# Adaptive average pooling on one core: every load issued as two transfers of 64 partitions each

## The chip, the cores and the metric

The kernel runs on one core of a Trainium2 chip. The metric is the device time of one execution in microseconds; the median of 3 timed runs of the kernel before is 333.51 us (333.32 to 333.81).

## The reference

The input `x` is float32 of 32 x 256 x 4096. Each row of 4096 values is cut into 256 windows, and each window is averaged:

```python
for i in range(output_size):                 # output_size = 256
    start = int(i * length / output_size)    # length = 4096
    end = int((i + 1) * length / output_size)
    result[:, :, i] = np.mean(x[:, :, start:end], axis=-1)
```

Since 4096 is a multiple of 256, each window has 16 values. The input is 134.2 MB, the output 8.4 MB.

## The kernel before

Batch and channels are flattened to 8,192 rows. A tile is 512 rows, 4 rows (64 KB) in each of the 128 partitions, so there are 16 tiles of 8.39 MB. For the first 15 tiles partition p owns the 60 rows from 60p on, and tile t takes rows 4t to 4t+3 of them (`x_many`); the last tile is the final 512 rows, 4 consecutive rows per partition (`x_last`). The tiles come from a pool `inpool` with two buffers, named `xin` in the profile.

For each tile, in the order of the loop:

- L73, SyncE's queue (SP): one DMA transfer loads the tile, 128 partitions x 64 KB. Its buffer is that of tile t-2, so the issue waits until the last reader of that buffer is done.
- L76, GpSimd (POOL): of the second half of the windows (512 of a partition's 1,024), it adds the last 8 values of each onto the first 8, in place.
- L81, VectorE (DVE): sums the first half of the windows over 16 values each. It waits for the load only.
- L84, VectorE: sums the second half of the windows over the 8 values that L76 left. It waits for POOL, and it is the last reader of the buffer.
- L87, ScalarE (ACT): multiplies the tile's 1,024 sums per partition by 1/16, in place.

Results are collected in `res_many` (15 tiles) and `res_last` (the last tile). The stores go through `store` (L58), also on SP's queue: `res_many` in one transfer of 7,680 KB, issued behind the last load, and `res_last` at the end in two, of 120 and of 8 partitions. All transfers are issued by SP, in the order of the program, to one DMA queue. Semaphores and waits are put in by the framework, by what an instruction reads and writes; the order within each engine is that of the program.

Of the kernel before, what the change touches and what calls it, by code (L numbers as in the profile page):

```python
# [1 line left out]

# [4 lines left out]


@with_exitstack
def kernel(  # L10
    ctx: ExitStack,
    tc: tile.TileContext,
    x: bass.AP,
    output_size: int,
    out: bass.AP,
):

    nc = tc.nc
    F32 = mybir.dt.float32
    X = mybir.AxisListType.X

    batch, channels, length = x.shape
    ob, oc, olen = out.shape
    assert ob == batch and oc == channels and olen == output_size
    assert length % output_size == 0
    window = length // output_size  # L30
    hw = window // 2
    inv_w = 1.0 / float(window)

    P = nc.NUM_PARTITIONS
    R = 4
    rows = batch * channels
    assert rows % (P * R) == 0
    ntiles = rows // (P * R)
    many = (ntiles - 1) * R
    cells = R * output_size  # L40
    m = cells // 2
    cols = R * length

    xr = x.rearrange("b c l -> (b c) l")
    orow = out.rearrange("b c o -> (b c) o")
    x_many = xr[0 : P * many, :].rearrange("(p r) l -> p (r l)", p=P, r=many)
    o_many = orow[0 : P * many, :].rearrange("(p r) o -> p (r o)", p=P, r=many)
    x_last = xr[P * many :, :].rearrange("(p r) l -> p (r l)", p=P, r=R)
    o_last = orow[P * many :, :].rearrange("(p r) o -> p (r o)", p=P, r=R)

    res_many = nc.alloc_sbuf_tensor("res_many", [P, (ntiles - 1) * cells], F32, align_bytes=256)
    res_last = nc.alloc_sbuf_tensor("res_last", [P, cells], F32, align_bytes=256)
    inpool = ctx.enter_context(tc.tile_pool(name="inpool", bufs=2))

    stored = nc.alloc_semaphore("stored")

    def store(out, in_):
        ins = nc.sync.dma_start(out=out, in_=in_)  # L58
        tc.no_tile_sem_insts.add(ins.ins.name)
        ins.then_inc(stored, 16)  # L60

    for t in range(ntiles):
        last = t == ntiles - 1
        xbuf = inpool.tile([P, cols + 64], F32, name="xin")
        off = 32 if last else 0
        flat = xbuf[:, off : off + cols]
        xin = flat.rearrange("p (o w) -> p o w", w=window)
        if last:
            res, base, src = res_last, 0, x_last
        else:  # L70
            res, base = res_many, t * cells
            src = x_many[:, t * cols : (t + 1) * cols]
        nc.sync.dma_start(out=flat, in_=src)  # L73
        if last:
            store(o_many, res_many[:, :])
        nc.gpsimd.tensor_add(  # L76
            out=xin[:, m:cells, 0:hw],
            in0=xin[:, m:cells, 0:hw],
            in1=xin[:, m:cells, hw:window],
        )  # L80
        nc.vector.reduce_sum(  # L81
            out=res[:, base : base + m], in_=xin[:, 0:m, :], axis=X
        )
        nc.vector.reduce_sum(  # L84
            out=res[:, base + m : base + cells], in_=xin[:, m:cells, 0:hw], axis=X
        )
        nc.scalar.mul(  # L87
            out=res[:, base : base + cells],
            in_=res[:, base : base + cells],
            mul=inv_w,  # L90
        )
    for lo, hi in ((0, 120), (120, P)):
        store(o_last[lo:hi, :], res_last[lo:hi, :])

    ctx.pop_all().close()
    tc.close()
    tc.compile()  # L97
    nc.sync.wait_ge(stored, 48)
    nc.sync.sem_clear(stored)


# [1 line left out]
_INS = ['x', 'output_size']  # L103
_OUTS = [((32, 256, 256), 'float32')]

_NUMBERS = {'output_size': 256}


# [26 lines left out]
```

## Time and profile before

| | |
|---|---|
| median of 3 runs | 333.51 us (333.32 to 333.81) |
| span of the profiled execution | 332.2 us, so the median lies 1.3 us above it |
| busy: DVE, POOL, ACT | 209.7 us (63%), 139.7 us (42%), 18.2 us (5%) |
| DMA | 142.61 MB in 2,599 packets, 99.4% of 16 engines' span |
| L76 (POOL), L81 (DVE), L84 (DVE), L87 (ACT), each per tile | 8.72, 8.69, 4.42, 1.06 us |
| issue of a load on SP (L73), median | 0.33 us |

The profile is that of one execution, and the time of that execution is known by its span; what lies around the span is the difference to the timed runs. In timeline lines the columns are start and duration in us, then engine, line, operation, what is written and read, and in brackets how long the engine idled before and what released it. In a table of stretches, each line has a window, its length, then for DVE, ACT and POOL the busy time with the number of instructions, the granted clock of TensorE (which is not used here), the mean busy share of the 16 DMA engines and the GB/s that they moved. "Landing" of a load is the moment at which its readers are released.

### The profile page before, as it was taken

To read this page: it belongs to the slowest core of one execution; us is meant where nothing else is said; L and a number is where in the kernel's file an instruction comes from. 1 tells how busy PE (TensorE), PEld (TensorE's weight loads), DVE (VectorE), ACT (ScalarE), POOL (GpSimd) and SP (SyncE) were. 2 spreads that over 40 slices of the span, in tenths; PEclk is the share of its full clock that TensorE was granted. 3 is DMA by queue.
4 is the path that set the end of the run, shared out by engine and by line. 5 is a ranking of instruction groups with operands and counts; after the bars stand their busy time and mean duration, and the time that the engine had idled before them with its cause. 6 is when DMAs were issued, how large, how long until landed. Compare 5 with 4: busy or idle time off the path is not lost.

```text
span 332.2 us, 160 instructions
## 1 busy us (share of the span) xinstructions
DVE 209.7 (63%) x32; ACT 18.2 (5%) x17; POOL 139.7 (42%) x20
## 2 busy tenths in 40 slices
DVE  0029396692939669392956939295683929578392
ACT  1000101000010100001010000101000010101001
POOL 0027090642709064370906337090633709063370
DMA  9898989989898999989898998989899998989897
GB/s 379 379 505 379 505 379 442 442 379 505 379 505 379 481 402 402 481 379 505 379 497 387 466 418 379 505 379 505 379 489 395 418 466 379 505 379 505 363 473 300
DMA packets 2599, 142.61 MB, mean 429 GB/s; under 512 B 295, under 2 KB 295, under 8 KB 423
## 3 DMA queue, kind: packets, MB, share of 16 engines
q1 hardware_dynamic: 2599, 142.61, 99.4%
HBM read 134.22 MB, written 8.39 MB: 429 GB/s over the span
## 4 chain that ended last, share of the span: by engine, by line
DMA 66%; POOL 18%; DVE 11%; POOLq 3%; issue 0%; ACT 0%; SPq 0%
DMA xin<-in_x_dram 66%; POOL xin L76 18%; DVE res_many L84 9%; POOLq L97 3%; DVE res_last L84 1%; ACT res_last L87 0%; SPq L73 0%; POOLq L76 0%
## 5 line engine op out<-in xcount | busy, mean ns | idle before, releaser
L76 POOL TENSOR_TENSOR xin<-xin 128x4096 f32<-128x4096 f32 x16 | 139.5, 8719 | 181.9 <-DMA xin<-in_x_dram 181.9
L81 DVE TENSOR_REDUCE res_many<-xin 128x512 f32<-128x8192 f32 x15 | 130.3, 8686 | 107.3 <-DMA xin<-in_x_dram 107.3
L84 DVE TENSOR_REDUCE res_many<-xin 128x512 f32<-128x4096 f32 x15 | 66.3, 4420 | 2.5 <-POOL xin L76 2.3
L87 ACT ACTIVATE res_many<-res_many 128x1024 f32<-128x1024 f32 x15 | 15.8, 1056 | 289.6 <-DVE res_many L84 289.6
L81 DVE TENSOR_REDUCE res_last<-xin 128x512 f32<-128x8192 f32 x1 | 8.7, 8686 | 6.6 <-DMA xin<-in_x_dram 6.6
L84 DVE TENSOR_REDUCE res_last<-xin 128x512 f32<-128x4096 f32 x1 | 4.4, 4420 | 0.2 <-POOL xin L76 0.2
L87 ACT ACTIVATE res_last<-res_last 128x1024 f32<-128x1024 f32 x1 | 1.1, 1056 | 18.8 <-DVE res_last L84 18.8
L87 ACT ACT_TABLE_LOAD x1 | 1.3, 1283 | 0.7 <-PEq L116 0.7
L116 POOL MEMSET const-float32-0.0<- 128x1 f32 x1 | 0.1, 99 | 0.2 <-issue 0.2
L116 POOL MEMSET const-bfloat16-1.0<- 128x1 bf16 x1 | 0.1, 102 | 0.0
L116 POOL MEMSET const-uint8-127<- 128x1 uint8 x1 | 0.1, 102 | 0.0
L116 POOL MEMSET const-float32-1.0<- 128x1 f32 x1 | 0.1, 99 | 0.0
## 6 DMA issues: line engine op xcount, KB each, us to landing
out_dram<-res_many SPq DMA_DIRECT2D x1, 7680.0 KB
out_dram<-res_last SPq DMA_DIRECT2D x1, 480.0 KB
xin<-in_x_dram SPq DMA_DIRECT2D x16, 25.3
out_dram<-res_last SPq DMA_DIRECT2D x1, 32.0 KB
```

Source lines behind the costliest of these rows:

```text
L76: nc.gpsimd.tensor_add(out=xin[:, m:cells, 0:hw], in0=xin[:, m:cells, 0:hw], in1=xin[:, m:cells, hw:window],)
L81: nc.vector.reduce_sum(out=res[:, base : base + m], in_=xin[:, 0:m, :], axis=X)
L84: nc.vector.reduce_sum(out=res[:, base + m : base + cells], in_=xin[:, m:cells, 0:hw], axis=X)
L87: nc.scalar.mul(out=res[:, base : base + cells], in_=res[:, base : base + cells], mul=inv_w,)
L97: tc.compile()
L116: nc = _bacc.Bacc("TRN2", target_bir_lowering=False, num_devices=1)
```

## The change

L73 issues two transfers instead of one: the first fills partitions 0 to 63 of the buffer, the second partitions 64 to 127. Bytes, buffers, order of the tiles and all compute instructions stay as they are. Lines below it move down by one, so L76, L81, L84 and L87 become L77, L82, L85 and L88, and the load is L74.

```diff
-        nc.sync.dma_start(out=flat, in_=src)
+        for a, b in ((0, P // 2), (P // 2, P)):
+            nc.sync.dma_start(out=flat[a:b, :], in_=src[a:b, :])
         if last:
             store(o_many, res_many[:, :])
```

## The prediction

> **What bounds the kernel now.** I read the page first: engine shares, DMA queue, chain.
>
> ```profile
> span 332.2 us, 160 instructions
> DVE 209.7 (63%) x32; ACT 18.2 (5%) x17; POOL 139.7 (42%) x20
> DMA packets 2599, 142.61 MB, mean 429 GB/s; under 512 B 295, under 2 KB 295, under 8 KB 423
> q1 hardware_dynamic: 2599, 142.61, 99.4%
> DMA xin<-in_x_dram 66%; POOL xin L76 18%; DVE res_many L84 9%; POOLq L97 3%; DVE res_last L84 1%; ACT res_last L87 0%; SPq L73 0%; POOLq L76 0%
> ```
>
> DVE works 63% of the span and POOL 42%, but the one DMA queue fills 99.4% of 16 engines' time. The chain names POOL and DVE for some 30%, because load t+2 is issued only when tile t has been reduced and its buffer is free. The question is whether that issue is ever late. The timeline and the stretches between landings answer it.
>
> ```profile
> 22.53 8.69 DVE L81 TENSOR_REDUCE res_many<-xin 128x512 f32<-128x8192 f32 x1 [22.53 <-DMA xin<-in_x_dram]
> 35.78 19.62 SPq L73 DMA_DIRECT2D xin<-in_x_dram  x2
> 41.83 8.69 DVE L81 TENSOR_REDUCE res_many<-xin 128x512 f32<-128x8192 f32 x1 [6.08 <-DMA xin<-in_x_dram]
> 61.17 8.69 DVE L81 TENSOR_REDUCE res_many<-xin 128x512 f32<-128x8192 f32 x1 [6.13 <-DMA xin<-in_x_dram]
> 293.08 8.69 DVE L81 TENSOR_REDUCE res_many<-xin 128x512 f32<-128x8192 f32 x1 [6.02 <-DMA xin<-in_x_dram]
> 312.96 8.69 DVE L81 TENSOR_REDUCE res_last<-xin 128x512 f32<-128x8192 f32 x1 [6.59 <-DMA xin<-in_x_dram]
> ```
>
> ```profile
> 80.60:293.10 212.50, 144.15 (x23) 11.62 (x11) 95.91 (x11) 1.00 1.00 434
> 313.00:330.40 17.40, 13.06 (x2) 1.06 (x1) 8.72 (x1) 1.00 0.92 398
> 330.40:331.60 1.20, 0.00 (x0) 0.00 (x0) 0.00 (x0) 1.00 0.95 389
> ```
>
> Load 2 is issued at 35.78 and load 1 lands at 41.83: the queue has 6 us of work left when new work arrives. Landings follow each other every (293.08 - 22.53) / 14 = 19.325 us, which for 8.39 MB is 434 GB/s, at a DMA share of 1.00 (last two columns). Behind the last landing the queue still has the 7,680 KB store of `res_many`, at 398 GB/s to 330.4; the last two stores follow at 389 GB/s to 331.6. So the whole span is one queue that is never empty: what matters is what the change does to the rate of the queue, and nothing else.
>
> **The change, part by part.** The built program lists 32 transfers of 64 x 16384 on SP where it had 16 of 128 x 16384; every other engine has the same instructions in the same order. So the change does what it says.
>
> SP: 16 more issues at 0.33 us each (L73's median). The second issue of a pair has no waits of its own, and comes 0.33 us behind the first, into the 6 us of slack: nothing on the path. Behind the last pair stands only the `res_many` store, whose rows wait behind the loads in the same queue anyway. If the slack were gone the price would be 16 x 0.33 = 5.3 us.
>
> Waits: L81 and L76 now wait for two landings. Between landing and start there are 0.02 to 0.11 us now; one more wait of that size per tile lies inside the 6 us that DVE idles before every L81. On the last tile it delays the last two stores, which queue behind `res_many`: DVE, POOL and ACT are done at 327.33, about 3 us before that store's rows run out at 330.4. Nothing.
>
> More packets: 295 small packets are 16 loads x 16, the `res_many` store's 16, 15 for the 120-row store and 8 for the 8-row one: one end mark per transfer and DMA engine used. The split adds 16 per engine. In the trace's packet records a row of 64 KB starts 2.414 us after the row before it, and 2.420 us where a load's end mark lies between: 6 ns each, 0.1 us in all.
>
> Start and completion: load 0 is issued at 0.73 and read at 22.53, so 21.80 - 19.325 = 2.48 us pass in start and completion. If none of it overlapped, 16 more transfers would cost 16 x 2.48 = 39.7 us; if the queue pipelines them as it pipelines loads now (cadence equal to the moving time), nothing. I take nothing, since two loads are already queued back to back without a gap.
>
> The rate of a 64-row transfer is the unknown. No transfer in the trace has 64 rows. Bounds from the nearest rows: a full load takes 19.325 us, 16 engines carrying 8 rows each, 27.1 GB/s an engine. If each engine keeps that pace with 4 rows per half, a half takes 9.66 us and the change costs nothing. If a transfer to half of the partitions has half of the ways into the memory, the 16 engines share them two by two, and a half takes the full 19.325 us: the bytes are halved and the time is not. The nearest smaller transfer is the 120-row store: 389 GB/s with 15 of 16 engines, against 15/16 of 434 = 407. That says that rate follows how much of the machine a transfer spans, but it is near the full end and cannot say which resource counts. A gain from the rate is excluded: the share is already 1.00 at 434.
>
> I take the upper end. At 128 rows each engine fills its own eight partitions without being slowed (2.42 us for nearly every row), which is what one separate way per engine looks like; with 64 rows the same 16 engines crowd on half of the partitions, and both halves run in order through the same queue, so the other half's ways stand empty meanwhile. All engines start together and get equal work, so nothing in the trace pulls them out of step.
>
> The Trainium skill, "SBUF — State Buffer", section "Door 1: The DMA port swizzle", says just this: partitions 0 to 63 reach only 8 of 16 DMA ports, with 196 GB/s measured at 1 MiB against 328 for 128 partitions; as an estimate from that page, its limit of about 218 GB/s would make the 134 MB of loads 616 us. "DMA: Bandwidth & Descriptors", "Rules for kernel authors", advises against two transfers to disjoint halves: they serialize. The trace agrees with those pages on the full-width rate (434 beside their 436), and shows no transfer that tests the half.
>
> The sum: 16 loads x 19.325 us more = 309.2. The tail of stores is unchanged. The span goes from 332.2 to 641.4; the timed median is 1.3 us above the span (333.51), so 642.7, and with the little that engines started some tenths of a microsecond apart may overlap, 642.
>
> **The rivals.**
>
> Not slower, 0.22: the destination sets no limit, each DMA engine does, and 4 rows + 4 rows are 8 rows. For it: the flat 27.1 GB/s an engine looks like the engine's own speed; and the tail at 389 GB/s shows no slow stretch although its last store has only 8 partitions, served by 8 engines at once. Against: that is 32 KB, which may be read ahead, and it is a store. Decided by whether two engines can write one group of partitions at full pace. Then 333.5 + 0.1 = 333.6, nothing in the chain moved, within the 0.2% (0.67 us) that a measurement here can tell from none.
>
> Partly overlapped, 0.13: the ways are halved, but one engine of a sharing pair gets ahead by half a load (9.66 us), and then the two work on opposite halves without meeting. Against: the lead cannot last. Load t+2 is issued when L84 of tile t ends, 13.2 us after the landing (41.83 to 55.06), so an engine 9.66 us ahead has run dry and waits 3.6 us, or up to 6.1 with 2.48 of start; call it 5. 333.5 + 9.7 + 15 x 5 = 418. It needs an uneven sharing between engines.
>
> Fixed cost not overlapped, 0.05: up to 39.7 us, so 334.3 to 373, if the queue starts a transfer only after the one before it has completed. Against it stands the cadence now.
>
> Faster, 0.10: the first half's rows start earlier, as a shorter transfer is described faster. What can shrink is part of load 0's 2.48 us; at most about 1 us, so 332.5. From then on the queue is one piece, so a start earlier by x ends earlier by x; it counts once x is over 0.67 us.
>
> **How the numbers follow.** Half rate 0.50, partly overlapped 0.13, fixed cost 0.05, no change 0.22, faster 0.10. Slower by over 0.2%: 0.68; within: 0.22; faster: 0.10. The likeliest case alone runs from 600 (a tenth of the sharing avoided) to 655 (sharing costs 4% in pace). The range of 8 in 10 has to reach down past 418 and 373 to the no-change case, as 0.50 + 0.18 is too little: 333.2 to 655, which leaves out the faster case, part of no change and the ends.
>
> **What would show it.** Landings of whole tiles (starts of L82 in the new numbering) 38.6 us apart, and a mean near 218 GB/s in the middle of the span with packets of twice the 2.42 us: the half rate. DVE's idle time before each tile would rise from 6 to about 25 us, and nothing else would grow. Landings still 19.3 apart with a share of 1.00 at 434 GB/s: no change, and my step on the ways into the memory is wrong. Landings of 24 us with packets of two lengths: partly overlapped. Normal packets with gaps between them: the fixed cost. The issue of the next pair later than the end of the running loads would prove the slack on SP wrong.

## The result and the profile after

The changed kernel takes 671.91 us (median of 4 runs, 671.35 to 672.98) against 333.62 us beside it: a ratio of 2.0148, 95% interval 2.0124 to 2.0172. The half rate that was forecast came, but 642 us was too little by 30 us, and the stated range ended at 655.

The page of the changed kernel: span and instructions, DVE, ACT and POOL, then the DMA totals with the queue's share of 16 engines, and the chain by line.

```profile
span 669.8 us, 194 instructions
DVE 209.7 (31%) x32; ACT 18.2 (3%) x17; POOL 139.7 (21%) x20
DMA packets 2855, 142.61 MB, mean 213 GB/s; under 512 B 551, under 2 KB 551, under 8 KB 679
q1 hardware_dynamic: 2855, 142.61, 99.8%
another core or an unknown queue 71%; POOL 20%; DMA 6%; POOLq 1%; DVE 1%; issue 0%; ACT 0%; SPq 0%
```

The engines do the same work to the tenth of a microsecond (209.7, 18.2, 139.7); the bytes are the same. The queue is as full as before (99.8%), at half the rate. There are 256 more small packets, 16 for each of the 16 additional transfers: every half is still carried by all 16 DMA engines. The chain's "another core or an unknown queue" is neither: where a reader waits for two loads, the view does not find the releaser. The idle times of the next view name it: the loads.

Timeline of the changed kernel (start, duration, engine, line, and in brackets the idle time before and its end):

```profile
44.00 8.69 DVE L82 TENSOR_REDUCE res_many<-xin 128x512 f32<-128x8192 f32 x1 [44.00 <-DMA xin<-in_x_dram]
84.44 8.69 DVE L82 TENSOR_REDUCE res_many<-xin 128x512 f32<-128x8192 f32 x1 [27.22 <-DMA xin<-in_x_dram]
610.28 8.69 DVE L82 TENSOR_REDUCE res_many<-xin 128x512 f32<-128x8192 f32 x1 [27.20 <-DMA xin<-in_x_dram]
650.63 8.69 DVE L82 TENSOR_REDUCE res_last<-xin 128x512 f32<-128x8192 f32 x1 [27.11 <-DMA xin<-in_x_dram]
```

and its stretches (last two columns: DMA share and GB/s):

```profile
84.40:610.30 525.90, 170.41 (x27) 13.73 (x13) 113.34 (x13) 1.00 1.00 207
650.60:669.80 19.20, 13.11 (x2) 1.06 (x1) 8.72 (x1) 1.00 0.89 386
```

A landing comes every (610.28 - 44.00) / 14 = 40.45 us instead of 19.325, DVE waits 27.2 us for each instead of 6, and from the last landing to the end it is 669.8 - 650.63 = 19.2 us, as before (332.2 - 312.96 = 19.2). All of the loss is in the loads: 16 x (40.45 - 19.325) = 338.0 us, and the span grew by 337.6.

### The profile page after: what moved, and what is told of

It is laid out like the page before. It is cut to its first block, busy times and chain, and to the rows that moved or that the text cites. A ratio compares the mean times of both kernels' runs of the same rounds, so it can differ in the third digit from the quotient of the medians.

```text
span 669.8 us, 194 instructions
## 1 busy us (share of the span) xinstructions
DVE 209.7 (31%) x32; ACT 18.2 (3%) x17; POOL 139.7 (21%) x20
## 3 DMA queue, kind: packets, MB, share of 16 engines
q1 hardware_dynamic: 2855, 142.61, 99.8%
HBM read 134.22 MB, written 8.39 MB: 213 GB/s over the span
## 4 chain that ended last, share of the span: by engine, by line
another core or an unknown queue 71%; POOL 20%; DMA 6%; POOLq 1%; DVE 1%; issue 0%; ACT 0%; SPq 0%
POOL xin L77 20%; DMA xin<-in_x_dram 6%; POOLq L98 1%; DVE res_last L85 1%; ACT res_last L88 0%; POOLq L77 0%; SPq L74 0%
## 5 line engine op out<-in xcount | busy, mean ns | idle before, releaser
L82 DVE TENSOR_REDUCE res_many<-xin 128x512 f32<-128x8192 f32 x15 | 130.3, 8686 | 425.0 <-DMA xin<-in_x_dram 425.0
L77 POOL TENSOR_TENSOR xin<-xin 128x4096 f32<-128x4096 f32 x16 | 139.5, 8718 | 519.5 <-DMA xin<-in_x_dram 519.5
L85 DVE TENSOR_REDUCE res_many<-xin 128x512 f32<-128x4096 f32 x15 | 66.3, 4421 | 1.9
L88 ACT ACTIVATE res_many<-res_many 128x1024 f32<-128x1024 f32 x15 | 15.8, 1056 | 606.8 <-DVE res_many L85 606.8
L82 DVE TENSOR_REDUCE res_last<-xin 128x512 f32<-128x8192 f32 x1 | 8.7, 8686 | 27.1 <-DMA xin<-in_x_dram 27.1
L85 DVE TENSOR_REDUCE res_last<-xin 128x512 f32<-128x4096 f32 x1 | 4.4, 4420 | 0.1
L88 ACT ACTIVATE res_last<-res_last 128x1024 f32<-128x1024 f32 x1 | 1.1, 1056 | 39.3 <-DVE res_last L85 39.3
```

The costliest lines, as they stand in the source:

```text
L77: nc.gpsimd.tensor_add(out=xin[:, m:cells, 0:hw], in0=xin[:, m:cells, 0:hw], in1=xin[:, m:cells, hw:window],)
L82: nc.vector.reduce_sum(out=res[:, base : base + m], in_=xin[:, 0:m, :], axis=X)
L85: nc.vector.reduce_sum(out=res[:, base + m : base + cells], in_=xin[:, m:cells, 0:hw], axis=X)
L88: nc.scalar.mul(out=res[:, base : base + cells], in_=res[:, base : base + cells], mul=inv_w,)
```

## The experiments

Four questions: is it the number of transfers, which partitions count, what two engines on one way cost, and does being out of step help. "Way" is used as in the prediction, for whatever lets a DMA engine into a part of the memory. "Row" is the piece that one partition gets in one transfer, 64 KB in most loads, and a "packet record" is the trace's entry for it, with its start and duration. The records do not name the engine; an engine's rows are found by the end of one meeting the start of the next, which gives 16 chains of equal length. Each kernel is the changed one with one edit, unless something else is said. The split by columns has ten times; all others have one each, and are read for effects far above the 0.2% by which times of one kernel differ.

**Two transfers by columns.** This kernel splits each load along the row, so both transfers have all 128 partitions.

```diff
-        for a, b in ((0, P // 2), (P // 2, P)):
-            nc.sync.dma_start(out=flat[a:b, :], in_=src[a:b, :])
+        for a, b in ((0, cols // 2), (cols // 2, cols)):
+            nc.sync.dma_start(out=flat[:, a:b], in_=src[:, a:b])
```

> Two transfers per load again, but both of all 128 partitions: the first half of each partition's 64 KB, then the second. Theory (two DMA engines that write the same eighth of the lower or upper 64 partitions share one way into the memory, so a transfer to partitions 0 to 63 has half of the ways): both halves use all ways, landings stay 19.3 us apart, time 333.5 to 334.2 us; the 16 additional transfers and the packets of half size cost some 0.1 to 0.6 us. Rival A (every transfer has a time of its own of about 20 us, whatever it moves): 40.4 us between landings, 670 us.

334.05 us against 333.37, ratio 1.0021 (1.0011 to 1.0030). Twice as many transfers cost 0.7 us, 0.4 to 1.0 by the interval. In the trace's packet records a 32 KB packet starts 1.209 us after the one before it, 5 ns more for two of them than the 2.414 us of a 64 KB packet; 8 more packets per engine and load make 16 x 8 x 5 ns = 0.64 us, which accounts for it. Rival A of the expectation, a time of its own for every transfer, is out.

**Partitions 32 to 95 as one transfer.**

```diff
-        for a, b in ((0, P // 2), (P // 2, P)):
+        for a, b in ((32, 96), (0, 32), (96, P)):
```

> Three transfers per load: partitions 32 to 95, then 0 to 31, then 96 to 127. If the half that matters is that of partition numbers (0 to 63 against 64 to 127), the 64 partitions from 32 to 95 lie on both sides, each engine has a way for itself there, and the two quarters are shared as before: 4 x 2.41 + 2 x (2 x 5.1) = 30.1 us per tile, span 16 x 30.1 + 22.6 = 504 us (22.6 is what the changed kernel's span of 669.8 leaves beside 16 x 40.45). Rival A (a time per transfer, 20.2 us each): 60.6 us per tile, 990 us. Rival B (any transfer of under 128 partitions runs at half pace, or reading 64 separate rows from memory does): 40.4 us per tile, 670 us or a little more.

515.81 us, span 514.2, 10 us more than worked out. Two landings and a middle stretch:

```profile
95.71 8.69 DVE L82 TENSOR_REDUCE res_many<-xin 128x512 f32<-128x8192 f32 x1 [17.82 <-DMA xin<-in_x_dram]
125.78 8.69 DVE L82 TENSOR_REDUCE res_many<-xin 128x512 f32<-128x8192 f32 x1 [16.80 <-DMA xin<-in_x_dram]
64.70:480.00 415.30, 183.46 (x28) 14.79 (x14) 122.06 (x14) 1.00 1.01 275
```

30.1 us between these two landings, as worked out, but 30.8 over all of them. In the packet records an engine's second to fourth row in the transfer of partitions 32 to 95 takes 2.42 us in seven of the sixteen tiles, and 2.71 to 2.79 in the other nine, which stays unexplained; rows of the two quarters take 4.4 to 5.1. So 64 partitions in one transfer can run at full pace, and none of their tiles comes near the half rate: it is not their number, nor the reading of 64 separate rows.

**Quarters, and sixteen partitions at a time.**

```diff
-        for a, b in ((0, P // 2), (P // 2, P)):
-            nc.sync.dma_start(out=flat[a:b, :], in_=src[a:b, :])
+        for a in (0, 32, 64, 96):
+            nc.sync.dma_start(out=flat[a : a + 32, :], in_=src[a : a + 32, :])
```

> Four transfers per load, of 32 partitions each in order. Theory: 32 partitions reach as many ways as the 64 that they belong to, so each 64 KB row takes about 5.1 us on two sharing engines: 4 x 2 x 5.1 = 41 us per tile, span 665 to 685 us. Rival A (a time per transfer): 81 us per tile, 1,315 us. Rival C (rate proportional to the partitions of a transfer: a quarter of the partitions, a quarter of the rate): 77 us per tile or more, 1,260 us.

671.91 us, span 670.6: four transfers of 32 partitions are as fast as two of 64. In the other kernel each transfer has 16 partitions (`range(0, P, 16)`, `a : a + 16`).

> Eight transfers per load, of 16 partitions each, one row per engine. By the theory 16 neighbouring partitions have 4 ways and 16 engines crowd on them four by four: 4 x 2.42 = 9.7 us a row without a loss, 10.3 with the loss of two sharers (6%), more if four sharers lose more; 8 rows: 77 to 85 us per tile, span 1,260 to 1,390 us. If all that counts is whether a transfer has fewer than 128 partitions: 40.4 us per tile, 670 us.

1,210 us, span 1,208.7: below the interval that I gave. Stretches of the two (quarters, then sixteen at a time):

```profile
84.40:610.00 525.60, 170.32 (x26) 13.73 (x13) 113.32 (x13) 1.00 1.00 208
```

```profile
151.50:1116.00 964.50, 170.36 (x26) 13.73 (x13) 113.33 (x13) 1.00 1.00 113
```

32 and 64 neighbouring partitions give 207 to 208 GB/s, 16 give 113, all 128 gave 434. If 16 neighbouring partitions have four ways, as the expectation assumes, a way carries 113 / 4 = 28 GB/s where four engines crowd on it; where two do, 207 / 8 = 26; one engine alone moves 27. So the price of sharing does not grow with the sharers: four have none. I had expected the loss of two to hold or to rise.

The Trainium skill, "SBUF — State Buffer", section "Door 1: The DMA port swizzle", has partitions 0 to 31 and 0 to 63 on the same 8 ports and 0 to 15 on four; the runs agree with the order (208, 207, 113). Its limit for 8 ports is about 218 GB/s, 5% above what two sharing engines reached here; here the measurement decides.

**Eight engines, each alone on its way.** Sixteen transfers per load, each of 8 partitions four apart.

```diff
-        for a, b in ((0, P // 2), (P // 2, P)):
-            nc.sync.dma_start(out=flat[a:b, :], in_=src[a:b, :])
+        for g in range(0, P, 32):
+            for a in range(g, g + 4):
+                nc.sync.dma_start(out=flat[a : g + 32 : 4, :], in_=src[a : g + 32 : 4, :])
```

> Each load as 16 transfers of 8 partitions, four apart (0, 4, ..., 28, then 1, 5, ..., 29, and so on for each block of 32). Eight rows go to eight DMA engines only, and no two of them write the same way, so each row should take 2.42 us alone: 16 x 2.42 = 38.7 us per tile, span about 642 us, although twice as few engines work. That is the half rate without the sharing: what lies between this and the changed kernel (40.45 us per tile, 669.8) is the price of two engines on one way. If eight engines on eight ways also lose 5% (the loss belongs to the ways, not to the sharing): 40.4 us per tile, 670. If the 16 ends of transfers per tile cost more than 0.1 us each, longer than 670.

645.52 us, span 644.2. Two landings, and the queue with its share:

```profile
80.98 8.69 DVE L83 TENSOR_REDUCE res_many<-xin 128x512 f32<-128x8192 f32 x1 [25.51 <-DMA xin<-in_x_dram]
119.70 8.69 DVE L83 TENSOR_REDUCE res_many<-xin 128x512 f32<-128x8192 f32 x1 [25.51 <-DMA xin<-in_x_dram]
q1 hardware_dynamic: 4391, 142.61, 51.4%
```

38.72 us between these landings (38.8 over all) with the share at 51%: eight engines in place of sixteen, eight times as many transfers as the changed kernel has, and still 1.7 us per tile faster. A row takes 2.42 us in the packet records, against 4.86 for the first row of a half and 5.12 for the next three in the changed kernel. So the half rate is worth 38.7 us per tile, as forecast, and having two engines on a way is worth the other 1.7.

**Even and odd partitions.**

```diff
-        for a, b in ((0, P // 2), (P // 2, P)):
-            nc.sync.dma_start(out=flat[a:b, :], in_=src[a:b, :])
+        for a in (0, 1):
+            nc.sync.dma_start(out=flat[a:P:2, :], in_=src[a:P:2, :])
```

> Two transfers per load, of the even partitions and of the odd ones. Each spans all ways of both halves. If it counts which ways the whole transfer reaches: 19.3 us per tile, 333 to 336 us. If it counts which rows the engines write at the same moment, and each engine has four successive rows of the transfer (partitions 8e, 8e+2, 8e+4, 8e+6), then at any moment only every other way is in use, two engines on each: about 40 us per tile, 655 to 672 us.

334.18 us against 333.55 beside it, span 332.6:

```profile
80.60:293.10 212.50, 144.16 (x22) 11.62 (x11) 95.91 (x11) 1.00 1.00 434
```

The same count of transfers, partitions and bytes as the changed kernel, and the full rate. What counts is which partitions are in work together. My second case, with neighbouring rows on one engine and pairs that meet, didn't come, and nearly all rows take 2.42 us from each engine's second one on, so no pair had to come out of step first: how the queue deals the rows of a strided transfer to the engines, or which partitions share a way, is not as I assumed there.

**A store in halves.** The kernel before, with only the `res_many` store split.

```diff
-            store(o_many, res_many[:, :])
+            for a, b in ((0, P // 2), (P // 2, P)):
+                store(o_many[a:b, :], res_many[a:b, :])
...
-    nc.sync.wait_ge(stored, 48)
+    nc.sync.wait_ge(stored, 64)
```

> The kernel before with whole loads; only the store of res_many is issued as two transfers, of partitions 0 to 63 and 64 to 127. If sharing a way costs reads out of the memory as it costs writes into it, the store takes twice its 18 us (and the loss): 333.5 + 18 to 20 = 352 to 354 us. If only writes into it are limited (the last store of the kernel before, 8 partitions on 8 engines, showed no slow stretch): 333.5 us.

352.05 us against 333.55, span 350.7. The stretch behind the last landing:

```profile
313.00:331.00 18.00, 12.92 (x2) 1.06 (x1) 8.64 (x1) 1.00 1.00 218
```

This is one store of 7.9 MB, and 18.5 us are lost on it. The GB/s of so short a stretch are rough, here 218 and 398 for the whole store, as a row counts where it starts. The packet records are plainer: from its first row's start to its last row's end the whole store takes 18.7 us, with 2.27 us for a row of 60 KB, and the two halves take 37.2, with 4.8 us for about half of the rows. So reads out of the memory are halved as writes into it are.

**Engines out of step.** Ahead of all loads, one transfer that only some of the DMA engines take part in.

```diff
+    nc.sync.dma_start(out=res_many[0:8, :], in_=x_many[0:8, 0 : (ntiles - 1) * cells])
     for t in range(ntiles):
```

> The changed kernel with one more transfer ahead of all loads: 8 rows of 60 KB into partitions 0 to 7 of res_many (overwritten later), which occupies only the first 8 of the 16 DMA engines. By the theory those 8 rows crowd on two ways, so it takes about 9 us, and the first 8 engines then lag by nearly half a load behind the other 8. If an engine shares its way with the one 8 places on, the two work on opposite halves and do not meet, until the leading one runs dry because the next load is issued only 13.2 us after a landing; about half of the lead survives that: some 29 to 31 us per tile, span near 500 us. Without a part of the lead lasting: 670 + 10 us. If sharing is not what halves the rate (rivals A, B, C): 672 to 682 us.

682.15 us, span 680.6. The added transfer of 480 KB is issued at 0.73 and landed at 12.27, when ScalarE starts:

```profile
12.27 1.28 ACT L89 ACT_TABLE_LOAD   x1 [12.27 <-DMA res_many<-in_x_dram]
93.04 8.69 DVE L83 TENSOR_REDUCE res_many<-xin 128x512 f32<-128x8192 f32 x1 [27.39 <-DMA xin<-in_x_dram]
620.89 8.69 DVE L83 TENSOR_REDUCE res_many<-xin 128x512 f32<-128x8192 f32 x1 [27.37 <-DMA xin<-in_x_dram]
```

So 8 neighbouring partitions were about as slow as expected (7.0 to 8.3 us a row in the packet records), and after that nothing was gained: landings (620.89 - 93.04) / 13 = 40.6 us apart. Yet the lead lasted: by the packet records eight engines run 3 to 4 us behind the other eight for the rest of the span, and all rows take 4.9 to 5.1 us all the same. That leaves two readings: sharing is not what halves the rate, for which I had written 672 to 682 us, or both partners were delayed alike. Two smaller versions delay 4 and 2 engines (`res_many[0:16:4, :]` and `res_many[0:8:4, :]`, same rows of `x_many`):

> The changed kernel with 4 rows of 60 KB ahead of the loads, into partitions 0, 4, 8 and 12 of res_many, which go to the first 4 DMA engines and delay these by 2.3 us. Which engines share a way is open: delaying the first 8 left the pace as it was, so both partners were delayed alike. If an engine's partner is 4 places on, four of the eight pairs now stand 2.3 us apart and the packet records show rows of 3 to 4 us at each change of the half for 8 engines; the time stays near 671 us as the other pairs set the end. If the partner is the neighbour (or 2 places on), rows stay at 4.9 and 5.1 us throughout: 672 us.

> The same with 2 rows, into partitions 0 and 4, which delay the first 2 DMA engines by 2.3 us. If neighbours share, nothing comes apart: 4.9 and 5.1 us throughout, 672 us. If the partner is 2 or 4 places on, two pairs come apart: 4 engines with rows of 3 to 4 us at each change of the half.

679.96 and 678.02 us, spans 678.4 and 676.4: 9 and 6 us longer than I had written, as an added row took 4.5 to 6.4 us instead of 2.3 while the first rows of the loads were in work beside it. In both, rows of the loads stay at 4.9 to 5.1 us behind the start, which by what I wrote says "neighbours share". It does not fit: in the run with 2 engines, one of them is 2 us or more away from every other engine in the records, so for 2 us around each change of the half no partner can be writing the same half as it does, and its rows there still take 4.9 and 5.1 us. Sharing between two engines, at the moment at which both write, does not explain that. Which engines share, and what holds one back whose partner has moved on, stays open.

**Two queues.** The upper half of each load is issued by ScalarE, on its own queue. The cut shows the issue alone; the loop around it is rebuilt as well, so that the loads of tiles 0 and 1 are issued ahead of it and those of tile t+2 behind ScalarE's work on tile t:

```diff
-        for a, b in ((0, P // 2), (P // 2, P)):
-            nc.sync.dma_start(out=flat[a:b, :], in_=src[a:b, :])
+        for q, a, b in ((nc.sync, 0, P // 2), (nc.scalar, P // 2, P)):
+            q.dma_start(out=flat[a:b, :], in_=src[a:b, :])
```

> The changed kernel with the upper half of each load (partitions 64 to 127) issued by ScalarE on its own queue, two tiles ahead on both queues, so that both halves of a tile are in work at once. If a DMA engine takes rows of the two queues in turn and keeps one row in work at a time, all engines go from half to half together: 5.1 us a row, 40 us per tile, 670 us. If the two queues bring the engines out of step, so that at a time about half of them write each half: rows of 2.42 to 3 us, 335 to 420 us.

650.3 us, span 648.7, (590.77 - 82.22) / 13 = 39.1 us between landings:

```profile
82.22 8.69 DVE L84 TENSOR_REDUCE res_many<-xin 128x512 f32<-128x8192 f32 x1 [25.88 <-DMA xin<-in_x_dram]
590.77 8.69 DVE L84 TENSOR_REDUCE res_many<-xin 128x512 f32<-128x8192 f32 x1 [25.89 <-DMA xin<-in_x_dram]
q1 hardware_dynamic: 1575, 75.50, 51.4%
q10 hardware_dynamic: 1280, 67.11, 48.4%
82.20:600.00 517.80, 179.49 (x28) 13.73 (x13) 122.05 (x14) 1.00 1.00 215
```

Both queues are in work for the whole span, each with half of the 16 engines' time, and the rate goes from 207 to 215 GB/s. The packet records show the first of my two cases: every engine takes a row of one queue and then a row of the other, and the 16 do so within about 1 us of each other, so most of the time all of them still write the same half. But a row takes 4.9 us instead of 5.1, as the first row of a half does in the changed kernel (4.86). So in both runs a row that follows one of the other half pays almost none of the price of sharing; why, no run shows. Nothing of the half rate is given back.

## Why the prediction was right in kind and wrong in size

**The half rate, right.** The upper end was taken for a 64-row transfer, 19.325 us for a half. Its reason was fewer ways for the same engines. The middle partitions, the even and odd ones and the quarters bear out that the partitions decide: pace follows which partitions are in work together, not the number of transfers or of partitions. In all these kernels a partition goes with its own place in the input, so by themselves they do not part the two ends of a transfer. The last tile does in part: its rows lie 64 KB apart in the input instead of 960 KB, and it lands 650.63 - 610.28 = 40.35 us behind the one before, like the others. That the engines meet on a way two by two is not shown: the runs out of step speak against the simple picture.

**The failing term: the pace of two engines that share.** The sum priced it at 2 x 2.414 us a row, twice the undisturbed pace, with nothing for sharing itself, and took a little off for engines that start apart. The range was to allow 4% in pace, but was worked out wrong: 655 is 4% on the added 309 us, while the slower pace holds for all 16 x 38.65 = 618 us of loads, which makes 24.7 us, or 667. Measured: 5.12 us for three rows of four and 4.86 for the first, so a half takes 4.86 + 3 x 5.12 = 20.2 us, 4.7% more than 19.325. 16 x (40.45 - 38.65) = 28.8 us; the sum before that deduction was 642.7, and 671.9 - 642.7 = 29.2. The kernel with one engine per way has 38.72 us per tile and a span of 644.2, against 641.4 in the sum, so the rest of the sum held.

**A reason that did not matter: "nothing pulls them out of step".** It spoke against the partly overlapped rival. It held in the changed kernel, where the engines stay within 1.2 us of each other, but it was not what kept the rate down: engines were pulled out of step in three runs, by 3 us and more of the 20 of a half, and nothing overlapped. The price of that rival, 418 us, was built on a mechanism that these runs don't show at all.

**The rival of no change.** It rested on the last store of the kernel before, 8 partitions on 8 engines without a slow stretch. In its packet records a row of 4 KB indeed takes 0.16 us, as in the store of 120 partitions before it. The split store shows that large stores are slowed all the same. Why 8 rows of 4 KB are not, no run shows; as a sign for loads of 64 KB a row they misled.

**What was hidden, right.** The issues on SP cost more than assumed, 0.58 us each (median of L74) instead of 0.33, all of it in slack that grew to some 27 us (the last pair is issued from 583.11 on, and the loads before it land at 610.28). The second wait and the tail cost nothing: 19.2 us behind the last landing in both. More transfers as such cost next to nothing: 0.7 us by columns, about as much in the one run with even and odd partitions. The other rivals were not seen: no fixed cost per transfer, and no earlier start, as the first row of load 0 starts 2.05 us into the span instead of 1.75.

## What to carry to other kernels

When a load or store is cut in two, cut it along the row, or so that each part spreads over all partitions; not into the lower and the upper half, which here halved the rate of loads and of a store alike. An idle queue is not the sign of this: the share stayed at 99.8%, and only the GB/s beside it, 207 instead of 434, told of the loss. And where a sum halves a shared resource, leave room for the price of sharing itself; here it was 5% on every load, 29 us, more than the whole margin of 13.

## What the runs showed of the hardware that was not expected

- 64 partitions at full rate: even ones alone (434 GB/s), and partitions 32 to 95 in seven of sixteen tiles (2.42 us a row, 2.71 to 2.79 in the others).
- Sixteen engines on 64 or 32 neighbouring partitions lose 5% against eight (207 GB/s, where eight engines carry 8.39 MB in 38.72 us, 217 GB/s); on 16 partitions they lose nothing more (113 GB/s). Where each engine's rows go to the two halves in turn, nearly all of the 5% is gone (215 GB/s).
- Two queues did not bring the two halves into work side by side: each engine took a row of one queue and then one of the other, all engines nearly in step.
- Engines 2 to 4 us out of step ran no faster than engines in step.
- SP's issue of a 64-row transfer of 64 KB rows takes 0.58 us, of a 128-row one 0.33.
